# A mixture-of-experts tail on one core: another order of the eight experts, and the token dispatches moved into the short ones

## The chip, the cores and the metric

One core of a Trainium2 chip runs the whole program in one launch. The metric is the device time of one execution in microseconds. The kernel before took 1400.51 us (median of 3 runs, 1397.81 to 1400.72). A core has TensorE (PE in the profile; its weight loads are PEld), VectorE (DVE), ScalarE (ACT), GpSimd (POOL), SyncE (SP, which here issues nearly all transfers) and 16 DMA engines that move data from HBM to the on-chip memory.

## The reference

The program is a two-layer transformer block over 256 tokens of width 1024 in float32. Layer 0 has a mixer and a dense feed-forward part, layer 1 another mixer and a mixture of experts. The change lies in the mixture alone. A router picks 2 of 8 experts for each token; each expert is a gated feed-forward network of width 3584, applied to the tokens that chose it, and the results are added with the router's weights:

```python
logits = jnp.dot(xt, w_router) + b_router
top_logit, top_e = lax.top_k(logits, TOP_K)          # TOP_K = 2
gate = jax.nn.softmax(top_logit, axis=-1)
...
h = x_pad[toks]                                      # tokens of expert e
return (jax.nn.silu(h @ w_gate[e]) * (h @ w_up[e])) @ w_down[e]
...
y = jnp.zeros((N + 1, D), F32).at[slot_tok].add(y_slots * slot_gate)[:N]
```

The result is added to the scaled residual and goes through a last layer norm. Which expert has how many tokens is known only at run time.

## The kernel before

**Experts in turn.** All weights of all eight experts are read, 3 matrices of 1024 x 3584 in float32 for each. They come in loads of 512 KB (128 partitions x 1024 floats): 28 each of gate, up and down weights, 84 loads an expert and 672 in all. Expert 0 is called N here (`None` in the code). The other seven are sorted by their token counts at run time, and are called by rank, 0 with the most tokens to 6 with the fewest. `ORDER` (line 985) is the order in which they are computed.

**Short and long ones.** Experts in `FEW` (line 986: N and ranks 3 to 6) are computed with room for 64 tokens, straight from the float32 weights: the two halves of the stationary operand's 64 columns go side by side, gate in one and up in the other (`gate_up_small`, `down_small`). They are called short here. Ranks 0, 1 and 2, the long ones, have room for 128 tokens, and each weight tile is split into a high part by ScalarE (`wh`, line 150) and a low part by VectorE (`wl`, line 152), of which TensorE makes three products (`mm3`, lines 164 to 166).

**Chunks.** `experts` (line 1198) goes through an expert in four chunks of the width 3584 (1024, 1024, 1024, 512). In each chunk it computes gate and up (`pgu`, or `pg` and `pu`), and then the down product `y` of the chunk before. So the last four down loads of an expert are used after the first sixteen gate and up loads of the next one, and the next expert's second chunk also holds the `combine` (line 1179) that adds the finished expert to the sum.

**Dispatch.** Before an expert can start, its tokens must be gathered on TensorE: a matrix of zeros and ones `d` picks them out of the tokens (`xeps`), with a few transposes (`dps`) and the router's weights (`gp`). `dispatch` (line 1002) does it for one or two long experts, `dispatch_small` (line 1041) for a short one. The dictionary in line 1243 says after the second chunk of which expert (by place in `ORDER`) which others (by place too) are dispatched. While TensorE does that, it takes no weights.

**The order on the engines.** `products_in_order` (line 60) fixes TensorE's order to the order of the code; the other engines' order comes from a scheduler. SyncE issues the loads in the order in which TensorE uses them.

**The buffers.** A load goes to one of 25 buffers in turn (4 of `NRAW`, 21 of `NRAW2`; ten more of another pool are lent once, at the start). It is issued when the buffer's last user is done: a matmul for a short expert, VectorE's `wl` for a long one. So SyncE can be at most 25 loads ahead of what has been used up.

Of the kernel before, what the change touches and what calls it, by code (L numbers as in the profile page):

```python
# [8 lines left out]
F32 = mybir.dt.float32  # L9
# [8 lines left out]
P = 128  # L18
# [21 lines left out]
def hybrid_kernel(ctx, tc, x, ev_w_in, ev_w_out, dif_lambda, dif_subln, ffd_w_gate, ffd_w_up, ffd_w_down,  # L40
# [6 lines left out]
    def mkpool(name, bufs=1, side="left", **kw):  # L47
        return tc.tile_pool(name=name, bufs=bufs, side=side, reuse_waits="tile", **kw)
# [10 lines left out]
    @contextmanager  # L59
    def products_in_order():  # L60

        traced = nc.cur_bb.bb.instructions
        last = traced[-1]
        yield
        start = next(k for k in reversed(range(len(traced))) if traced[k] is last) + 1
        todo = [i for i in traced[start:] if i.engine == mybir.EngineType.PE]
        for a, b in zip(todo, todo[1:]):
            tc.add_manual_dep(b, a.name, mybir.DependencyInfo(mybir.DependencyClass.NoSync,
                                                              mybir.DependencyReason.DATA), reason="in order")
# [67 lines left out]
    def behind(ins):  # L137
        return tc.issue_after(ins) if ins is not None else nullcontext()
# [183 lines left out]
    def evac(dst, src):  # L322
        flip[0] ^= 1
        if flip[0]:
            nc.scalar.copy(dst, src)  # L325
        else:
            nc.vector.tensor_copy(dst, src)  # L327
# [355 lines left out]
    with tc.issue_after(turned):  # L683
# [15 lines left out]
        for q in range(4):  # L699
            r = slice(q * 32, q * 32 + 32)  # L700
# [240 lines left out]
    mp = ctx.enter_context(mkpool("moe"))  # L941

    def trb(shape, name):
        return tr.tile(list(shape), F32, tag="tr", name=name)
# [37 lines left out]


    SMALL = 64
    ORDER = (None, 0, 3, 1, 4, 2, 5, 6)
    FEW = (None, 3, 4, 5, 6)

    MORE = [(r, SMALL if r in FEW else P) for r in ORDER] + [(None, SMALL + P)]
    over = mp.tile([P, len(MORE) + 1], F32, name="over")
# [9 lines left out]
    def columns(r):  # L999
        return (posm[:, :, 0:1], weight[:, :, 0:1]) if r is None else (posr[:, :, r:r + 1], weightr[:, :, r:r + 1])  # L1000

    def dispatch(rs):


        n = len(rs)
        d = mp.tile([P, NT, 2, P], F32R, tag="d", name="d", bufs=1)
        for t in range(NT):
            for i, (r, base) in enumerate(rs):
                nc.vector.tensor_scalar(d[:, t, i], iota, float(base - 4096), columns(r)[0][:, t],
                                        op0=ALU.add, op1=ALU.is_equal)  # L1010
        xe = []
        for src, nm in ((xh, "xeh"), (xl, "xel")):
            dst = [mp.tile([P, KD, P], F32R, tag=nm, name=nm, bufs=2) for _ in range(n)]
            for k0 in range(0, KD, 2):
                ps = trb((P, 2, n, P), "xeps")
                for k in range(2):
                    for t in range(NT):
                        nc.tensor.matmul(ps[:, k], src[:, t, (k0 + k) * P:(k0 + k + 1) * P], d[:, t, :n],
                                         start=t == 0, stop=t == NT - 1)
                for i in range(n):  # L1020
                    evac(dst[i][:, k0:k0 + 2], ps[:, :, i])
            xe.append(dst)
        ps = trb((P, 4, P), "dps")
        for i in range(n):
            for t in range(NT):
                nc.tensor.transpose(ps[:, 2 * i + t], d[:, t, i].bitcast(F32), ident)
        gp = trb((P, 2), "gp")
        for i, (r, base) in enumerate(rs):
            for t in range(NT):
                nc.tensor.matmul(gp[:, i:i + 1], d[:, t, i].bitcast(F32), columns(r)[1][:, t],  # L1030
                                 start=t == 0, stop=t == NT - 1)
        gs = mp.tile([P, 2], F32, tag="gs", name="gs", bufs=3)
        nc.vector.tensor_copy(gs[:, :n], gp[:, :n])
        res = {}
        for i, r in enumerate(rs):
            dT = mp.tile([P, NT, P], F32R, tag="dT", name="dT", bufs=4)
            evac(dT, ps[:, 2 * i:2 * i + 2])
            res[r] = ([(xe[0][i][:, k], xe[1][i][:, k]) for k in range(KD)], gs[:, i:i + 1], dT)
        return res

    def dispatch_small(r, first):


        d = mp.tile([P, NT, P], F32 if first else F32R, tag="d", name="d_s", bufs=1)
        for t in range(NT):
            for h in range(2):
                last = nc.vector.tensor_scalar(d[:, t, h * SMALL:(h + 1) * SMALL], iota[:, 0:SMALL], -4096.0,
                                               columns(r)[0][:, t], op0=ALU.add, op1=ALU.is_equal)
        marks["d"] = last.ins
        xs = mp.tile([P, KD, SMALL], F32, tag="xs", name="xs", bufs=2)  # L1050
        srcs = (x3,) if first else (xh, xl)
        for k0 in range(0, KD, 4):
            ps = trb((P, 4, SMALL), "xeps")
            for k in range(4):
                for t in range(NT):
                    for j, src in enumerate(srcs):
                        nc.tensor.matmul(ps[:, k], src[:, t, (k0 + k) * P:(k0 + k + 1) * P], d[:, t, 0:SMALL],
                                         start=t == 0 and j == 0, stop=t == NT - 1 and j == len(srcs) - 1)
            evac(xs[:, k0:k0 + 4], ps)
        gp = trb((P, 1), "gp")  # L1060
        for t in range(NT):
            nc.tensor.matmul(gp, d[:, t].bitcast(F32), columns(r)[1][:, t], start=t == 0, stop=t == NT - 1)
        gs = mp.tile([P, 2], F32, tag="gs", name="gs", bufs=3)
        nc.vector.tensor_copy(gs[:, 0:1], gp)
        ps = trb((P, NT, P), "dps")
        for t in range(NT):
            nc.tensor.transpose(ps[:, t], d[:, t].bitcast(F32), ident)
        dT = mp.tile([P, NT, P], F32R, tag="dT", name="dT", bufs=4)
        evac(dT, ps)
        return {(r, 0): (xs, gs[:, 0:1], dT)}  # L1070
# [4 lines left out]
    def weights_of(e):  # L1075

        ws = (moe_w_gate, moe_w_up, moe_w_down)
        if isinstance(e, int):
            return [w[0, e] for w in ws]
        return [w[0, bass.ds(e, 1)].rearrange("o d f -> (o d) f") for w in ws]  # L1080
# [117 lines left out]
    def experts(runs, groups, small, disp):  # L1198

        turns, pend = [], []  # L1200

        def mid():
            while turns:
                turns.pop(0)()

        for p, (r, base) in enumerate(runs):
            if r is None:
                e = 0
            else:
                with behind(loads[-1] if p else None):  # L1210
                    e = nc.values_load(idxi[0:1, r:r + 1], engines=(mybir.EngineType.SP,), min_val=1, max_val=NE - 1)
            ws = weights_of(e)
            sm = r in small
            xe, gs, dT = disp.pop((r, base))
            ys = [yp.tile([P, 512], F32, tag="y", name="y") for _ in range(1 if sm else 2)]
            for i, (c0, n) in enumerate(CHUNKS):
                hs = (gate_up_small if sm else gate_up)(ws, c0, n, xe, mid)
                for f in pend:
                    f()
                ts = []  # L1220
                turns.append(lambda ts=ts, hs=hs, sm=sm: ts.extend((turn_small if sm else turn)(hs)))
                pend = [lambda ws=ws, c0=c0, n=n, ts=ts, ys=ys, sm=sm: (down_small if sm else down)(ws, c0, n, ts, ys)]
                if i == 1:
                    for q in groups.get(p, ()):
                        if runs[q[0]][0] in small:
                            disp.update(dispatch_small(runs[q[0]][0], False))
                        else:
                            disp.update(dispatch([runs[n_] for n_ in q]))
            pend.append(lambda ys=ys, gs=gs, dT=dT, p=p: turns.append(
                lambda: combine(ys, gs, dT, p == 0 and bool(small))))  # L1230
        mid()
        for f in pend:
            f()
        mid()

    disp = dispatch_small(None, True)
# [3 lines left out]
        with tc.issue_after(marks["d"]):  # L1240
            nc.vector.tensor_tensor(xl[:, t], x3[:, t], xh[:, t].bitcast(F32), ALU.subtract)
    with products_in_order():
        experts([(r, 0) for r in ORDER], {0: ((1, 3),), 1: ((2,),), 3: ((4,),), 4: ((5,),), 5: ((6,),), 6: ((7,),)}, FEW, disp)
    def tokens_over(i):
        return nc.values_load(overi[0:1, i:i + 1], min_val=0, max_val=S)

# [8 lines left out]
    for t in (1, 0):  # L1255
        z = acc[:, t]
        mu, r = layer_stats(z)
# [50 lines left out]
```

## Time and profile before

| | |
|---|---|
| time, median of 3 runs | 1400.51 us |
| the profiled execution's own time | 1402.62 us |
| its span, first to last instruction | 1400.8 us |
| TensorE busy | 1314.0 us (94%) |
| VectorE, ScalarE busy | 754.3 us (54%), 544.7 us (39%) |
| read from HBM | 427.64 MB |
| the experts' part of the span | from about 519 us to about 1380 us |

The profile is of one execution. The page cuts the span in 40 slices of 35 us; in its row of GB/s, the slices of the experts' part read between 329 and 409. Times below are counted from the span's start. "Busy" for TensorE counts a matmul from its start to its modelled end, so matmuls that follow each other overlap, and a stretch can be busy though TensorE waits for weights.

### The profile page before, as it was taken

The numbers are of one execution on the slowest core, as the hardware profiler recorded it, in microseconds if no ns is written. First come the engines' busy times: TensorE is split into PE (matmuls) and PEld (weight loads), VectorE is DVE, ScalarE is ACT, GpSimd is POOL, SyncE is SP. The second block draws the span as 40 slices with busy tenths as digits, with TensorE's granted clock in tenths as the row PEclk, the third lists the DMA queues.
The fourth block names the chain that finished last, engine by engine and source line by source line (L and its number), as shares of the span: only waits on it lengthen the run. The fifth ranks groups of instructions, "written<-read, shape, count | busy, mean of one in ns | idle before, by whom it ended". The sixth has DMA issues, their size and how long they took to land. (4 is left out here: it accounts for less than half of the span.)

```text
span 1400.8 us, 18207 instructions
## 1 busy us (share of the span) xinstructions
PE 1314.0 (94%) x6136; PEld 848.2 (61%) x6136; DVE 754.3 (54%) x1194; ACT 544.7 (39%) x796; POOL 45.2 (3%) x79
## 2 busy tenths in 40 slices
PE   8979999998988989999999999999998999999983
PEld 7856888886864763367874356884446886432221
DVE  5977655547578561278863057893137895201004
ACT  4454444433436311166652056772034774100000
POOL 2200000001210000000000000000000000000000
PEclk9999999999999989999999999999999999999996
DMA  9244646545543399899999999999999998999992
GB/s 348 74 135 137 225 149 211 181 121 178 161 150 121 124 362 399 333 408 409 402 355 399 402 409 409 401 408 384 405 406 409 407 389 329 409 402 409 409 402 108
DMA packets 146805, 429.98 MB, mean 307 GB/s; under 512 B 15696, under 2 KB 23280, under 8 KB 146704
## 3 DMA queue, kind: packets, MB, share of 16 engines
q1 hardware_dynamic: 146000, 426.48, 80.3%
q0 software_dynamic: 704, 2.26, 0.5%
q8 instruction: 50, 0.82, 0.2%
q14 instruction: 51, 0.42, 0.1%
HBM read 427.64 MB, written 1.05 MB: 306 GB/s over the span
## 5 line engine op out<-in xcount | busy, mean ns | idle before, releaser
L152 DVE TENSOR_TENSOR wl<-raw,wh 128x1024 fp32r<-128x1024 f32 x378 | 456.0, 1225 | 116.0 <-ACT wh L150 113.0
L150 ACT CAST wh<-raw 128x1024 fp32r<-128x1024 f32 x378 | 390.1, 1046 | 230.1 <-PE pg L166 67.7
L1124 PE MATMUL pgu<-raw,xs 128*64 128x512 f32 x1120 | 267.4, 608 | 5.1 <-DMA raw<-in_moe_w_up_dram 4.3
L1124 PEld LDWEIGHTS pgu<-raw,xs 128*64 128x64 f32 x1120 | 81.7, 139 | 166.6 <-issue 130.1
L1169 PE MATMUL y<-raw,hT_s 128*64 128x512 f32 x560 | 132.9, 605 | 6.8 <-DMA raw<-in_moe_w_down_dram 5.9
L1132 DVE TENSOR_TENSOR h_s<-h_s,pgu 64x512 f32<-64x512 f32 x35 | 24.1, 690 | 185.3 <-ACT h_s L1131 185.1
L1169 PEld LDWEIGHTS y<-raw,hT_s 128*64 128x64 f32 x560 | 37.9, 138 | 95.3 <-issue 61.7
L1131 ACT ACTIVATE h_s<-pgu 64x512 f32<-64x512 f32 x35 | 20.7, 590 | 175.7 <-PE pgu L1124 175.7
L164 PE MATMUL mmps<-wh,xTh 128*128 128x512 f32 (+2 forms) x192 | 77.4, 404 | 1.0 <-ACT wh L150 0.8
L166 PE MATMUL mmps<-wh,xTl 128*128 128x512 f32 (+2 forms) x192 | 76.2, 399 | 1.8 <-DVE xTl L173 1.7
L165 PE MATMUL mmps<-wl,xTh 128*128 128x512 f32 (+2 forms) x192 | 75.0, 393 | 0.5 <-DVE wl L152 0.5
L164 PE MATMUL pg<-wh,xeh 128*128 128x512 f32 x168 | 71.0, 422 | 1.9 <-ACT wh L150 1.6
L165 PE MATMUL pg<-wl,xeh 128*128 128x512 f32 x168 | 69.3, 413 | 2.3 <-DVE wl L152 2.3
L166 PE MATMUL pg<-wh,xel 128*128 128x512 f32 x168 | 68.8, 409 | 0.0
L164 PE MATMUL y<-wh,hTh 128*128 128x512 f32 x168 | 66.6, 396 | 0.8 <-ACT wh L150 0.8
L165 PE MATMUL y<-wl,hTh 128*128 128x512 f32 x168 | 66.5, 396 | 0.9 <-DVE wl L152 0.8
L166 PE MATMUL pu<-wh,xel 128*128 128x512 f32 x168 | 66.8, 398 | 0.0
L165 PE MATMUL pu<-wl,xeh 128*128 128x512 f32 x168 | 66.7, 397 | 0.0
L166 PE MATMUL y<-wh,hTl 128*128 128x512 f32 x168 | 66.3, 394 | 0.0
L164 PE MATMUL pu<-wh,xeh 128*128 128x512 f32 x168 | 65.4, 389 | 0.0
L327 DVE COPY hT_s<-tps 128x256 f32<-128x256 f32 x17 | 7.2, 424 | 101.5 <-PE tps L1151 101.5
L325 ACT COPY hT_s<-tps 128x256 f32<-128x256 f32 x18 | 6.7, 372 | 135.1 <-PE tps L1151 135.1
(376 smaller groups left out, 1912.8 us busy)
## 6 DMA issues: line engine op xcount, KB each, us to landing
raw<-in_moe_w_up_dram SPq DMA_DIRECT2D x224, 512.0 KB, 10.1
raw<-in_moe_w_gate_dram SPq DMA_DIRECT2D x224, 512.0 KB, 10.1
raw<-in_moe_w_down_dram SPq DMA_DIRECT2D x224, 512.0 KB, 10.1
raw<-in_ffd_w_gate_dram SPq DMA_DIRECT2D x22, 512.0 KB, 5.1
raw<-in_ffd_w_up_dram SPq DMA_DIRECT2D x22, 512.0 KB, 4.4
raw<-in_ffd_w_down_dram SPq DMA_DIRECT2D x22, 512.0 KB, 4.7
raw<-in_ev_w_in_dram SPq DMA_DIRECT2D x20, 512.0 KB, 8.9
raw<-in_od_w_in_dram SPq DMA_DIRECT2D x20, 512.0 KB, 4.2
```

The source lines that it names most:

```text
L150: nc.scalar.copy(wh[:, :w], rv)
L152: nc.vector.tensor_tensor(wl[:, :w], rv, wh[:, :w].bitcast(F32), ALU.subtract)
L164: nc.tensor.matmul(ps, ah, wh, start=first and i == 0, stop=False)
L165: nc.tensor.matmul(ps, ah, wl, start=False, stop=False)
L166: nc.tensor.matmul(ps, al, wh, start=False, stop=last and i == n - 1)
L325: nc.scalar.copy(dst, src)
L327: nc.vector.tensor_copy(dst, src)
L1124: nc.tensor.matmul(p_[i * SMALL:(i + 1) * SMALL], xs[:, k0 + k], halves(w[k], n)[j], start=k0 + k == 0, stop=k0 + k == KD - 1)
L1131: nc.scalar.activation(h[:SMALL], p_[:SMALL], AF.Silu)
L1132: nc.vector.tensor_tensor(h[:SMALL], h[:SMALL], p_[SMALL:], ALU.mult)
L1169: nc.tensor.matmul(ys[0][i * SMALL:(i + 1) * SMALL], ts[k], w[:, i * 512:(i + 1) * 512], start=c0 == 0 and k == 0, stop=c0 + n == F_EXP an ...
```

## The change

Three edits. The order becomes N 3 0 4 1 5 2 6 instead of N 0 3 1 4 2 5 6: which experts are short and which long stays the same, and so does the last one. The dispatches move: N now hosts rank 3; rank 3 hosts ranks 0 and 1 together and then rank 4; rank 4 hosts rank 5 and then rank 2; rank 5 hosts rank 6. Before, N hosted 0 and 1, rank 0 hosted 3, rank 1 hosted 4, rank 4 hosted 2, rank 2 hosted 5, and rank 5 hosted 6. And the small tile `gs`, which holds an expert's router weights until it is combined, gets 5 buffers instead of 3.

```diff
-    ORDER = (None, 0, 3, 1, 4, 2, 5, 6)
+    ORDER = (None, 3, 0, 4, 1, 5, 2, 6)
...
-        gs = mp.tile([P, 2], F32, tag="gs", name="gs", bufs=3)
+        gs = mp.tile([P, 2], F32, tag="gs", name="gs", bufs=5)
...
     with products_in_order():
-        experts([(r, 0) for r in ORDER], {0: ((1, 3),), 1: ((2,),), 3: ((4,),), 4: ((5,),), 5: ((6,),), 6: ((7,),)}, FEW, disp)
+        experts([(r, 0) for r in ORDER], {0: ((1,),), 1: ((2, 4), (3,)), 3: ((5,), (6,)), 5: ((7,),)}, FEW, disp)
```

How this moves instructions is shown at three places of TensorE's order. The first is in expert N, after its second chunk; `d` is the matrix of a long expert's dispatch, `d_s` that of a short one, `x3h` and `x3l` are the two parts of the tokens. Before:

```order
L1169 MATMUL y<-raw,hT_s 64x512 x16
L1018 MATMUL xeps<-d,x3h 128x256 x16
L1018 MATMUL xeps<-d,x3l 128x256 x16
L1026 MATMUL dps<-ident,d 128x128 x4
L1030 MATMUL gp<-weightr,d 128x1 x4
L1124 MATMUL pgu<-raw,xs 64x512 x8
L1151 MATMUL tps<-ident,h_s 128x64 x8
```

The same place in the changed kernel, from the last of 32 `xeps` matmuls of rank 3's dispatch on:

```order
L1057 MATMUL xeps<-d_s,x3l 128x64
L1062 MATMUL gp<-weightr,d_s 128x1 x2
L1067 MATMUL dps<-ident,d_s 128x128 x2
L1124 MATMUL pgu<-raw,xs 64x512 x8
L1151 MATMUL tps<-ident,h_s 128x64 x8
```

The dispatch of two long experts has gone from here, and that of a short one stands in its place. The second place is in rank 4, after its second chunk. Before:

```order
L1124 MATMUL pgu<-raw,xs 64x512 x24
L1169 MATMUL y<-raw,hT_s 64x512 x16
L1018 MATMUL xeps<-d,x3h 128x128 x16
L1018 MATMUL xeps<-d,x3l 128x128 x16
L1026 MATMUL dps<-ident,d 128x128 x2
L1030 MATMUL gp<-weightr,d 128x1 x2
L1124 MATMUL pgu<-raw,xs 64x512 x8
```

The same place in the changed kernel, again from the last of the 32 on:

```order
L1057 MATMUL xeps<-d_s,x3l 128x64
L1062 MATMUL gp<-weightr,d_s 128x1 x2
L1067 MATMUL dps<-ident,d_s 128x128 x2
L1018 MATMUL xeps<-d,x3h 128x128 x16
L1018 MATMUL xeps<-d,x3l 128x128 x16
L1026 MATMUL dps<-ident,d 128x128 x2
L1030 MATMUL gp<-weightr,d 128x1 x2
L1124 MATMUL pgu<-raw,xs 64x512 x8
```

A short expert's dispatch has been put in ahead of the long one's, with no weights used in between. The third place is the middle of a long expert, between the second chunk's `pu` and `y` and the third chunk's `pg`. Before, in rank 0:

```order
L1057 MATMUL xeps<-d_s,x3l 128x64
L1062 MATMUL gp<-weightr,d_s 128x1 x2
L1067 MATMUL dps<-ident,d_s 128x128 x2
L164 MATMUL pg<-wh,xeh 128x512
L165 MATMUL pg<-wl,xeh 128x512
L166 MATMUL pg<-wh,xel 128x512
```

The same place in the changed kernel:

```order
L164 MATMUL y<-wh,hTh 128x512
L165 MATMUL y<-wl,hTh 128x512
L166 MATMUL y<-wh,hTl 128x512
L164 MATMUL pg<-wh,xeh 128x512
L165 MATMUL pg<-wl,xeh 128x512
L166 MATMUL pg<-wh,xel 128x512
```

No dispatch stands in a long expert any more: the third chunk follows the down products directly.

## Rows read from the trace of the kernel before

**Rows 1.** Windows: us; busy time (and count) by engine; PEclk, DMA share, GB/s

```profile
564.00:576.00 12.00, 12.00 (x65) 4.79 (x66) 1.66 (x7) 0.64 (x2) 0.00 (x0) 1.00 0.67 223
576.00:726.00 150.00, 148.47 (x671) 106.95 (x668) 111.19 (x109) 93.02 (x100) 0.00 (x0) 0.98 1.03 405
726.00:741.00 15.00, 15.00 (x71) 7.17 (x71) 3.17 (x4) 2.48 (x3) 0.00 (x0) 1.00 0.77 274
...
1160.00:1186.00 26.00, 26.00 (x117) 15.92 (x117) 13.12 (x12) 10.04 (x11) 0.00 (x0) 1.00 0.84 304
1186.00:1370.00 184.00, 172.16 (x742) 59.27 (x738) 22.73 (x36) 15.08 (x27) 0.00 (x0) 0.99 1.03 405
```

**Rows 2.** SyncE's longest wait in 555:572, then in 1160:1186 (total us, times, longest)

```profile
SPq L131 <- PE pgu L1124: 11.1, 2, 9.5
...
SPq L131 <- PE pgu L1124: 9.1, 5, 5.9
```

**Rows 3.** Timeline of TensorE: three dispatches (0 and 1; 2; 6), and what follows

```profile
556.56 1.22 PE L1018 MATMUL xeps<-d,x3h 128*128 128x256 f32 x8
...
564.68 3.65 PE L1124 MATMUL pgu<-raw,xs 128*64 128x512 f32 x16
...
997.47 2.29 PE L1018 MATMUL xeps<-d,x3h 128*128 128x128 f32 x16
...
1003.57 6.58 PE L1124 MATMUL pgu<-raw,xs 128*64 128x512 f32 x16
...
1220.75 0.30 PE L1057 MATMUL xeps<-d_s,x3h 128*128 128x64 f32 x1
...
1225.63 4.79 PE L1124 MATMUL pgu<-raw,xs 128*64 128x512 f32 x16
```

**Rows 4.** Timeline of TensorE: first weight matmuls of N, 0, 3, 1, 4, 2, 5, 6

```profile
518.83 4.91 PE L1124 MATMUL pgu<-raw,xs 128*64 128x512 f32 x16
...
600.75 0.50 PE L164 MATMUL pg<-wh,xeh 128*128 128x512 f32 x1
...
730.67 3.65 PE L1124 MATMUL pgu<-raw,xs 128*64 128x512 f32 x16
...
815.93 0.51 PE L164 MATMUL pg<-wh,xeh 128*128 128x512 f32 x1 [1.60 <-ACT wh L150]
...
949.88 2.37 PE L1124 MATMUL pgu<-raw,xs 128*64 128x512 f32 x10
...
1042.56 0.50 PE L164 MATMUL pg<-wh,xeh 128*128 128x512 f32 x1
...
1175.37 1.94 PE L1124 MATMUL pgu<-raw,xs 128*64 128x512 f32 x8
...
1262.73 3.60 PE L1124 MATMUL pgu<-raw,xs 128*64 128x512 f32 x16
```

**Rows 5.** Timeline of SyncE: issue of the first load of 3, 1, 4, 2, 5, 6

```profile
691.91 0.34 SPq L131 DMA_DIRECT2D raw<-in_moe_w_gate_dram  x1
...
804.36 0.33 SPq L131 DMA_DIRECT2D raw<-in_moe_w_gate_dram  x1
...
914.32 0.33 SPq L131 DMA_DIRECT2D raw<-in_moe_w_gate_dram  x1
...
1024.53 0.70 SPq L131 DMA_DIRECT2D raw<-in_moe_w_gate_dram  x1
...
1136.60 0.33 SPq L131 DMA_DIRECT2D raw<-in_moe_w_gate_dram  x1
...
1249.22 0.34 SPq L131 DMA_DIRECT2D raw<-in_moe_w_gate_dram  x1
```

**Rows 6.** Window behind rank 2's dispatch, columns as in the first rows

```profile
1003.60:1010.10 6.50, 6.50 (x18) 1.71 (x17) 0.81 (x5) 0.00 (x0) 0.00 (x0) 0.55 1.02 405
```

**Rows 7.** The last load of all: line 131 in 1363:1364, issue and landing

```profile
L131 SPq DMA_DIRECT2D raw<-in_moe_w_down_dram x1: 333/333/333, 1363.2 to 1363.2; - x1
...
DMA to landing us min/median/max: 11.5/11.5/11.5
```

More of the change, by code (lines that the diff above doesn't have):

```diff
@@ L1062, in dispatch_small @@
             nc.tensor.matmul(gp, d[:, t].bitcast(F32), columns(r)[1][:, t], start=t == 0, stop=t == NT - 1)
-        gs = mp.tile([P, 2], F32, tag="gs", name="gs", bufs=3)
+        gs = mp.tile([P, 2], F32, tag="gs", name="gs", bufs=5)
         nc.vector.tensor_copy(gs[:, 0:1], gp)
```

## The prediction

> **What bounds the kernel now.** I read the windows of the experts' part first, for the rate of the transfers. It is 405 GB/s in the long stretches, with a DMA share of 1.03, and 223, 274 and 304 GB/s in three short ones [rows 1]. TensorE's busy time cannot tell that: it is 172.16 of 184 us in the last stretch, where it follows the loads, and all of 26 us in one where it holds them up. So the bound is the stream of weights, 672 loads, and what can be won are the stretches in which it stalls. Against 405 GB/s they lose 12 x (1 - 223/405) = 5.4 us, 15 x (1 - 274/405) = 4.9 us and 26 x (1 - 304/405) = 6.5 us, 16.8 us in all [rows 1].
>
> Next SyncE's waits: in the first and the third of these stretches its longest waits, 9.5 and 5.9 us, are for a `pgu` matmul of TensorE [rows 2]. It waits for a buffer: it is 25 loads ahead, and TensorE has not used the oldest. The first stall comes while TensorE does the dispatch of ranks 0 and 1, from 556.56 to 564.68 us, and uses no weights for 8.1 us [rows 3]. The other two come where a short expert begins after a long one: rank 3 at 730.67 and rank 5 at 1175.37 us [rows 4].
>
> To see why there and not behind rank 1, I take for each expert the lead: from the issue of its first load [rows 5] to its first weight matmul [rows 4].
>
> - rank 3: 730.67 - 691.91 = 38.8 us, a stall of 4.9 us behind it
> - rank 1: 815.93 - 804.36 = 11.6 us; TensorE waits for the load here ("ACT wh", 1.60 us), so this is the floor
> - rank 4: 949.88 - 914.32 = 35.6 us, no stall
> - rank 2: 1042.56 - 1024.53 = 18.0 us
> - rank 5: 1175.37 - 1136.60 = 38.8 us, a stall of 6.5 us
> - rank 6: 1262.73 - 1249.22 = 13.5 us
>
> So up to 35.6 us the stream does not stall. The lead is cut off at 38.8 us, and what would go beyond turns into stall. An unhindered expert's 84 loads take 1024.53 - 914.32 = 110.2 us [rows 5]. TensorE needs more than that for a long expert (the lead grows) and less for a short one (it shrinks). For rank 2 the lead would have grown from 18.0 by 132.8 - 110.2 = 22.6 us to 40.6; it went with a stall of 6.5 us. Between the two points a stall of 6.5/(40.6 - 35.6) = 1.3 us belongs to each us above 35.6.
>
> **The change part by part.** First the prices of the dispatches [rows 3]: two long ones 564.68 - 556.56 = 8.1 us, one long 1003.57 - 997.47 = 6.1 us, one short 1225.63 - 1220.75 = 4.9 us. The matmuls that follow can be slow: 16 of them take 3.65 us at best, 4.79 after the short dispatch (1.1 more), 6.58 after the long one (2.9 more). All dispatches are the same in number and kind before and after, so only their places count.
>
> *The first stall.* N loses a dispatch of 8.1 us and gets one of 4.9 us. The buffer comes free 3.2 us earlier, less 0 to 1.1 us for slow matmuls: 2.2 to 3.3 us of the 5.4 stay. I take 2.7.
>
> *Rank 3 in the second place.* N takes 600.75 - 518.83 - 8.1 + 4.9 + 1.1 = 79.8 us, so rank 3 begins at 598.6 us. A short expert without a dispatch is 87.4 - 4.9 - 1.1 = 81.3 us (rank 5, 1175.37 to 1262.73, less its dispatch). With its two dispatches rank 3 takes at most 81.3 + 8.1 + 4.9 + 1.1 = 95.4 us, to 694.0 us. Rank 0's first load is the one now issued at 691.91 us, in the same place of the stream, 2.7 us earlier; with the floor of 11.6 us it is used at 700.8 us. So TensorE waits for loads, 6.8 us are to spare, the 13 us of dispatch cost nothing, and rank 0 begins at the floor. With that cover gone they would be paid in lead, one for one.
>
> *Rank 0, now without a dispatch.* Rank 2's 132.8 us less 4.9 are 127.9 us, so a long expert adds 17.7 us: from 11.6 to 29.3. No stall: 4.9 us saved.
>
> *Rank 4 with two dispatches.* It takes 92.7 us now (949.88 to 1042.56), with rank 2's dispatch and the slow matmuls in it. The short dispatch adds 4.9 to 6.0 us: 98.7 us, and the lead falls by 11.5, to 17.8. VectorE's rows for it stand ahead in its order or take under 1 us between the two; I leave that in the bound.
>
> *Rank 1* then ends at 17.8 + 17.7 = 35.5 us, just at the point where stalls begin. From below this costs 0; from above, if the second dispatch too ran at half speed (6.1 us more), 41.6 us and 1.3 x 6.0 = 7.8 us. I take 1.5, since the nearest row is rank 4's start now, at the same 35.6 us and without a stall.
>
> [...]
>
> *Rank 5, rank 2, rank 6.* Rank 5 takes off 110.2 - 87.4 = 22.8 (35.5 to 12.7), rank 2 adds 17.7 (30.4, no stall: 6.5 us saved), and rank 6 takes off 110.2 - 81.3 = 28.9, more than there is. So TensorE ends waiting for loads, as now, with the same last expert behind them. The tail from the last load's landing at 1363.2 + 11.5 = 1374.7 us [rows 7] to the end is not touched.
>
> *`gs` with 5 buffers* costs nothing on any queue; it lets four dispatched experts wait.
>
> The sum: stalls of 16.8 us become 2.7 + 0 + 1.5 + 0 = 4.2, a gain of 12.6 us. The profiled execution would go from 1402.62 to 1390.0 us. It lay 2.1 us above the median shown, so for that I say 1388.0 us.
>
> **The rivals.**
>
> *Given back behind rank 1.* The clock falls for the whole of rank 4's double dispatch: 7.8 us of stall in place of 1.5, so 1394.3. For it: [rows 6] and the lead of 35.5, which has no room. Against it: rank 5's dispatch slowed the next matmuls by 1.1 us alone.
>
> *No stall at all.* Long experts take less than 127.9 us once their middle is not broken: then rank 1's end lies below 35.6, and if the first stall goes too, the time is 1400.5 - 16.8 = 1383.7; with 2.7 of it left, 1386.4. For it: rank 0 now needs 129.9 us with its dispatch (600.75 to 730.67), 3 less than rank 2. Against it: rank 0 follows N, whose result is the first and is not added to a sum; all three long ones now follow a short expert whose is.
>
> *It doesn't do what it says.* If rank 3 does not run into its loads, rank 0 begins above the floor, and all leads behind it rise. It needs 13 us more there (6.8 to spare and 6.3 up to 35.6), and about 10 beyond for today's stalls: 1400. Nothing in the rows asks for 23 us in a short expert.
>
> *Slower: TensorE becomes the bound.* With two short experts first it idles early, and one short expert alone is left to catch up at the end. From 700.8 us it has 3 x 127.9 + 98.7 + 87.4 + 81.3 = 651.1 us to do, to 1351.9; the last load lands at 1374.7 - 12.6 = 1362.1. So 10 us are to spare. From 10 us of extra work on, the end moves with TensorE; from 23 on, the kernel is slower than before. Three long experts of 134 us (rank 1's time now, 815.93 to 949.88, with a dispatch) and 6 us in rank 4 would make 18 + 6 = 24: about 1402 us. Against it: 4.9 us of the 134 are the dispatch that leaves.
>
> **How the numbers follow.** The forecast 0.62, given back 0.20, no stall 0.08, not what it says 0.05, slower 0.05. What a measurement of this kernel can tell from no change is about 0.2%, 2.8 us. The first three are faster by more: 0.90; then the same 0.05 and slower 0.05. The range from 1383.5 (no stall) to 1396 (given back, with 1.5 us of run to run) leaves out the last two and little else.
>
> **What would show it.** In the profile after: a short low-rate stretch of about 2 to 3 us lost near 560 us; none where rank 4 and rank 6 begin; at most a small one where rank 5 begins (near 1050 us); rank 3 (second) with TensorE waiting for loads before rank 0 starts near 701 us; leads near 29, 35 and 30 us at the ends of ranks 0, 1 and 2; rates near 405 GB/s from 700 us on; and the last load landing near 1362 us. I am wrong if a stall of 5 us stands behind rank 1 or inside rank 4, if rank 0 starts well after 701 us, or if TensorE does not wait for loads in rank 6's last chunks.

## The result, and the profile after

The changed kernel takes 1390.28 us (median of 5 runs, 1388.07 to 1393.63) against 1400.72 us: ratio 0.9923, 95% interval 0.9906 to 0.994. It is faster, by 10.4 us; 1388.0 us had been forecast. Its profiled execution is the longest of the five: 1393.63 us, a span of 1391.9 us. A later set gave the same kernel 1391.35 us against 1399.53 (0.9941, 0.992 to 0.9962).

The windows of the kernel after (columns as in [rows 1]) show where the stream of weights still stalls:

```profile
562.00:578.00 16.00, 16.00 (x76) 5.52 (x74) 1.60 (x3) 1.55 (x3) 0.00 (x0) 0.91 0.86 310
...
890.00:906.00 16.00, 15.98 (x72) 6.83 (x73) 2.08 (x8) 0.74 (x2) 0.00 (x0) 0.82 0.64 216
906.00:1057.00 151.00, 148.14 (x650) 104.86 (x646) 108.61 (x102) 90.91 (x99) 0.00 (x0) 0.98 1.03 407
1057.00:1070.00 13.00, 13.00 (x63) 4.55 (x64) 0.69 (x1) 0.58 (x1) 0.00 (x0) 1.00 0.89 331
1070.00:1340.00 270.00, 260.24 (x1192) 151.12 (x1190) 136.38 (x140) 110.20 (x127) 0.00 (x0) 0.99 1.03 407
```

Against 405 GB/s they lose 16 x (1 - 310/405) = 3.8 us at N's dispatch, 16 x (1 - 216/405) = 7.5 us inside rank 4 and 13 x (1 - 331/405) = 2.4 us behind rank 1. Behind rank 0 and rank 2, where [rows 1] had 4.9 and 6.5 us, nothing is lost. SyncE's waits in the three places (555 to 575, 885 to 905, 1055 to 1070 us; total, times, longest) have the same partner as in [rows 2]:

```profile
SPq L131 <- PE pgu L1124: 12.2, 5, 8.2
...
SPq L131 <- PE pgu L1124: 13.2, 4, 10.7
...
SPq L131 <- PE pgu L1124: 8.3, 6, 4.8
```

The middle one is new, and longer than those of [rows 2]. TensorE's timeline at the four dispatch places, answering to [rows 3], shows why (N; rank 3, two long and then a short one; rank 4, a short and then a long one; rank 5):

```profile
554.37 0.30 PE L1057 MATMUL xeps<-d_s,x3h 128*128 128x64 f32 x1
559.41 6.31 PE L1124 MATMUL pgu<-raw,xs 128*64 128x512 f32 x16
...
644.97 1.21 PE L1018 MATMUL xeps<-d,x3h 128*128 128x256 f32 x8
653.64 0.39 PE L1057 MATMUL xeps<-d_s,x3h 128*128 128x64 f32 x1 [0.51 <-DVE d_s L1047]
661.91 6.26 PE L1124 MATMUL pgu<-raw,xs 128*64 128x512 f32 x16
...
878.64 0.30 PE L1057 MATMUL xeps<-d_s,x3h 128*128 128x64 f32 x1
884.13 3.67 PE L1018 MATMUL xeps<-d,x3h 128*128 128x128 f32 x16 [0.38 <-DVE d L1009]
892.63 5.26 PE L1124 MATMUL pgu<-raw,xs 128*64 128x512 f32 x16
...
1105.04 0.30 PE L1057 MATMUL xeps<-d_s,x3h 128*128 128x64 f32 x1
1109.63 3.65 PE L1124 MATMUL pgu<-raw,xs 128*64 128x512 f32 x16
```

Rank 4's two dispatches take 892.63 - 878.64 = 14.0 us, rank 3's 661.91 - 644.97 = 16.9 us. The windows of rank 4's, and of the 16 matmuls behind them, have the clock:

```profile
878.60:892.60 14.00, 13.61 (x78) 12.77 (x76) 3.19 (x9) 2.23 (x6) 0.00 (x0) 0.63 0.94 370
892.60:897.90 5.30, 5.30 (x18) 1.52 (x19) 0.81 (x5) 0.00 (x0) 0.00 (x0) 0.69 0.14 29
```

The granted clock is 0.63 and 0.69, and while those 16 matmuls run, the loads all but stop: 29 GB/s. So the place to look at is not only the start of an expert but also where TensorE takes up its weights again behind a dispatch. A low GB/s alone is not yet a loss of that size, as the second profile below shows; here the loads behind the pause did land late.

First-load issues and first weight matmuls of ranks 0, 4, 1 and 5, as [rows 5] and [rows 4]:

```profile
686.84 0.33 SPq L131 DMA_DIRECT2D raw<-in_moe_w_gate_dram  x1
...
795.89 0.33 SPq L131 DMA_DIRECT2D raw<-in_moe_w_gate_dram  x1
...
911.64 0.33 SPq L131 DMA_DIRECT2D raw<-in_moe_w_gate_dram  x1
...
1019.86 0.34 SPq L131 DMA_DIRECT2D raw<-in_moe_w_gate_dram  x1
```

```profile
700.59 0.50 PE L164 MATMUL pg<-wh,xeh 128*128 128x512 f32 x1
...
827.75 3.65 PE L1124 MATMUL pgu<-raw,xs 128*64 128x512 f32 x16
...
930.29 0.50 PE L164 MATMUL pg<-wh,xeh 128*128 128x512 f32 x1
...
1057.01 3.65 PE L1124 MATMUL pgu<-raw,xs 128*64 128x512 f32 x16
```

The leads are 13.8, 31.9, 18.7 and 37.2 us. From rank 4's first load to rank 1's pass 911.64 - 795.89 = 115.8 us, 5.6 more than the 110.2 that [rows 5] gave for an unhindered expert, and 6.7 and 7.5 more than the 109.1 and 108.2 us of ranks 0 and 1 here. One wait has grown besides: behind each of the three long experts TensorE idles before its last down products (5.0 us on ScalarE in three waits), since ScalarE does the short expert's silu ahead of the casts for them. Before, one such wait of 0.79 us on ScalarE is in the trace. The one in rank 4:

```profile
844.09 0.49 PE L164 MATMUL y<-wh,hTh 128*128 128x512 f32 x1 [1.65 <-ACT wh L150]
845.35 0.79 PE L165 MATMUL y<-wl,hTh 128*128 128x512 f32 x1 [0.77 <-DVE wl L152]
```

The down products behind it run at a granted clock of 0.57 (844 to 849 us).

The last load is issued at 1354.1 us and lands 11.5 us later ([rows 7]: 1363.2 and 11.5). The part ahead of the experts differs by some us from one execution to the next, so I measure from N's first weight matmul to the last landing: 855.9 us before (518.83 to 1374.7), 850.2 after (515.41 to 1365.6).

### The profile page after: what moved, and what is told of

Same layout as the page of the kernel before. It is cut to its first block, busy times and chain, and to the rows that moved or that the text cites. A ratio compares the mean times of both kernels' runs of the same rounds, so it can differ in the third digit from the quotient of the medians.

```text
span 1391.9 us, 18210 instructions
## 1 busy us (share of the span) xinstructions
PE 1306.8 (94%) x6136; PEld 851.5 (61%) x6136; DVE 753.0 (54%) x1194; ACT 543.4 (39%) x796; POOL 48.9 (4%) x79
## 5 line engine op out<-in xcount | busy, mean ns | idle before, releaser
L1124 PE MATMUL pgu<-raw,xs 128*64 128x512 f32 x1120 | 260.9, 614 | 0.0
L1169 PE MATMUL y<-raw,hT_s 128*64 128x512 f32 x560 | 127.6, 595 | 5.1 <-DMA raw<-in_moe_w_down_dram 3.5
```

The costliest lines, as they stand in the source:

```text
L1124: nc.tensor.matmul(p_[i * SMALL:(i + 1) * SMALL], xs[:, k0 + k], halves(w[k], n)[j], start=k0 + k == 0, stop=k0 + k == KD - 1)
L1169: nc.tensor.matmul(ys[0][i * SMALL:(i + 1) * SMALL], ts[k], w[:, i * 512:(i + 1) * 512], start=c0 == 0 and k == 0, stop=c0 + n == F_EXP an ...
```

## The experiments

The theories they set against each other: A, TensorE's work is paid only up to the last place where the stream waits for it, and a stall that goes earlier comes back there; B, each stall is a loss of its own; C, the moved dispatches carry the gain; E, the clock falls. This table has all runs. "Stretch" is the time from N's first weight matmul to the last landing in the one profiled execution. Each ratio is to the kernel before as timed in the same set (medians of 1399.07 to 1400.72 us). The sets did not all run on the same chip, so the ratios compare kernels of different sets better than the medians do. Of the edits to line 1243 the dictionary alone is shown below; a key in brackets is (place, chunk), both counted from 0, and goes with the change of the code shown for N's dispatch.

| kernel | stretch, us | median, us (runs) | ratio to before, 95% |
|---|---|---|---|
| before | 855.9 | 1400.72 (5) | |
| after | 850.2 | 1390.28 (5) | 0.9923 (0.9906 to 0.994) |
| after, again | 843.2 | 1391.35 (9) | 0.9941 (0.992 to 0.9962) |
| order only | 844.5 | 1391.16 (6) | 0.9943 (0.9924 to 0.9963) |
| dispatches only | 859.9 | 1406.92 (6) | 1.0058 (1.0041 to 1.0075) |
| N's dispatch later | 841.9 | 1391.21 (6) | 0.9946 (0.9926 to 0.9966) |
| two dispatches later | 842.4 | 1388.01 (6) | 0.9913 (0.9893 to 0.9933) |
| pairs split | 843.4 | 1388.98 (5) | 0.9914 (0.9893 to 0.9936) |
| rank 4's dispatch doubled | 851.6 | 1397.19 (12) | 0.9985 (0.9968 to 1.0002) |
| rank 6's doubled | 854.3 | 1397.54 (12) | 0.9982 (0.9962 to 1.0002) |
| split and late | 841.1 | 1387.14 (5) | 0.9906 (0.989 to 0.9922) |
| two buffers less | 847.4 | 1396.31 (11) | 0.9984 (0.9968 to 1.0) |
| casts first | 842.9 | 1389.45 (6) | 0.9927 (0.9907 to 0.9947) |
| late, rank 5's doubled | 843.2 | 1388.77 (6) | 0.9928 (0.9909 to 0.9948) |

### Which half of the change: the order alone, the dispatches alone

```
order only (in after):
-    {0: ((1,),), 1: ((2, 4), (3,)), 3: ((5,), (6,)), 5: ((7,),)}
+    {0: ((1,),), 1: ((2, 4),), 2: ((3,),), 3: ((6,),), 4: ((5,),), 6: ((7,),)}
dispatches only (in before; gs with 5 buffers):
-    {0: ((1, 3),), 1: ((2,),), 3: ((4,),), 4: ((5,),), 5: ((6,),), 6: ((7,),)}
+    {0: ((1, 3), (2,)), 2: ((4,),), 4: ((5,), (6,)), 6: ((7,),)}
```

> The new order, but the short experts' dispatches put back into the long experts ahead of them (rank 4's into rank 0, rank 5's into rank 1, rank 6's into rank 2); the two long ones, ranks 0 and 1, stay in rank 3. Theory A (one path): TensorE works without a gap from N's start to the end of the last stall, and then the loads that are left set the end; only how much of TensorE's work lies before that point counts. Then the order alone carries nearly all of the gain: no stall inside rank 4, since it starts at a lead near 35 us with one long dispatch, as before the change, where it had none; a stall of about 8 us behind rank 1, whose lead grows by rank 5's dispatch to some 42 us; 3.8 us at N's dispatch. Sum 11.8 us against 13.2 us after the change: 1389 us (1386 to 1392). Theory C (the moved dispatches carry the gain, each long expert that loses one saves 5 us of stall): about 1396 us or more.

> The order of before (N 0 3 1 4 2 5 6), but the short experts' dispatches moved into short experts: rank 3's from rank 0 to N, rank 4's from rank 1 to rank 3, rank 5's from rank 2 to rank 4, where rank 2's stands already. Theory A (one path): every dispatch that moves was before the last stall (behind rank 2) and still is, so the stalls change places and little in sum: 5 us more at N's dispatches, 4 us less behind rank 0, 7 us new inside rank 4, 6.5 us less behind rank 2. 1402 us (1399 to 1406). Theory C (the moved dispatches carry the gain): 1390 to 1394 us.

The order alone has the whole gain, 1391.16 us. Its stalls did not come where A had put them: rank 5 started at a lead of 34.0 us, not 42, and the window behind rank 1 (348 GB/s over 16 us) lost 2.3 us, not 8. The dispatches alone are slower than before, by 0.6%: C falls. In that kernel N does a pair and a short one in a row, 16.4 us, and the loads stand still meanwhile:

```profile
560.00:576.00 16.00, 14.91 (x72) 11.26 (x74) 3.91 (x16) 1.96 (x6) 0.00 (x0) 0.68 0.12 46
```

That is 16 x (1 - 46/405) = 14.2 us lost where before lost 5.4. A's sum was 4.9 us short: I had counted 5 us more at N, and it is 8.8.

### Is a stall a loss of its own: N's dispatch later

```
-                if i == 1:
-                    for q in groups.get(p, ()):
+                if True:
+                    for q in groups.get((p, i), ()):
...
+    {(0, 2): ((1,),), (1, 1): ((2, 4), (3,)), (3, 1): ((5,), (6,)), (5, 1): ((7,),)}
```

> The kernel after, with N's dispatch (of rank 3) traced in N's third chunk of four, not in its second. The stall of 3.8 us at 562 to 578 us goes in both theories. Theory B (stalls add up, each is a loss of its own): 1386.5 us, 3.8 us less than after. Theory A (one path): rank 3 ends when TensorE is through with N and rank 3, no earlier; the loads run 3 to 4 us further ahead, rank 0's lead grows from 13.8 to about 17 us and rank 4's from 31.9 to about 35 us, and the stall inside rank 4 grows by the same 3 to 4 us: 1390 us, no change within 1.5 us.

The stall at N's dispatch is gone from the profile, and the time is 1391.21 us, that of the kernel after. That speaks for A, but does not settle it. B's 1386.5 us takes off the 3.8 us of one execution; with the 2.5 us that the stall has in the second profile below, B says about 1389 us (from the 1391.35 of that set), which the interval of about 2.8 us either way leaves open. And the leads did not go A's way: rank 0 began at 11.2 us, the floor, not at 17, and rank 4 at 30.5, not 35.

### Where a dispatch costs nothing: two of them later

```
-    {0: ((1,),), 1: ((2, 4), (3,)), 3: ((5,), (6,)), 5: ((7,),)}
+    {0: ((1,),), 1: ((2, 4), (3,)), 3: ((5,),), 5: ((6,),), 6: ((7,),)}
```

> The kernel after, with two dispatches moved later: rank 2's from rank 4 to rank 5, rank 6's from rank 5 to rank 2. Rank 4 keeps rank 5's short one alone. Theory A (one path): some 9.4 us of dispatch and the slow matmuls behind it, 2 us, now come after the point of the last stall. No stall inside rank 4, rank 1 starts at a lead of about 14 us and ends at 31 to 32, no stall behind it; rank 5 with one long dispatch comes down to 15; rank 2 with rank 6's dispatch ends at 37 to 38, a stall of about 2 us behind it. 3.8 + 2 us of stall against 13.2: 1383 us (1381 to 1386). Theory D (not the dispatch: rank 4 stalls because of what follows a long expert there, the idle time of TensorE before the long expert's last down products and the slow matmuls): the stall inside rank 4 stays over 4 us and the time over 1387 us.

1388.01 us. Inside rank 4 and behind rank 1 no stall is left: rank 4 starts at a lead of 29.6 us and rank 1 at 11.2. Besides N's dispatch, one low place remains, where rank 6 starts at a lead of 34.6 us; a stall of about 2 us had been expected there:

```profile
1268.00:1284.00 16.00, 16.00 (x76) 6.23 (x76) 0.69 (x1) 0.63 (x2) 0.00 (x0) 1.00 0.86 322
```

D had the stall stay, and it is gone with the idle time before the down products still there, so D falls as it was put; the profile of casts first, below, has the dispatches and not the idle time, and no stall either. The gain is 2 to 3 us, not 7, and the time lies 2.0 us outside A's range: my 13.2 us of stall came from one execution that had more of it than most, as the next run shows.

### The same kernel again, and the pairs split

> The changed kernel once more, for a second profile of it and six more times. Every theory: 1390 us (1388 to 1393). What it is to show is which of its stretches differ from one execution to the next. Theory E (the clock falls by chance behind a single dispatch and always behind two in a row): the two double dispatches, in ranks 3 and 4, take 13 us or more again, and the 16 matmuls behind them over 5 us; the single ones in N and rank 5 take 4.6 to 5.9 us, with 3.65 us or over 5 us behind them, either.

In this execution the pair in rank 4 took 13.1 us and the lead at its start was 29.4 us. TensorE's timeline at N and rank 4, then the first-load issues of ranks 4 and 1 on SyncE, then the window behind the pair:

```profile
553.66 0.30 PE L1057 MATMUL xeps<-d_s,x3h 128*128 128x64 f32 x1
558.31 3.65 PE L1124 MATMUL pgu<-raw,xs 128*64 128x512 f32 x16
...
870.94 0.30 PE L1057 MATMUL xeps<-d_s,x3h 128*128 128x64 f32 x1
884.09 5.21 PE L1124 MATMUL pgu<-raw,xs 128*64 128x512 f32 x16
```

```profile
793.51 0.33 SPq L131 DMA_DIRECT2D raw<-in_moe_w_gate_dram  x1
...
903.70 0.33 SPq L131 DMA_DIRECT2D raw<-in_moe_w_gate_dram  x1
```

```profile
884.00:900.00 16.00, 16.00 (x73) 5.57 (x75) 1.23 (x6) 0.78 (x2) 0.00 (x0) 0.90 0.95 346
```

Behind N's dispatch the 16 matmuls take 3.65 us where they took 6.31: the same code, at a granted clock of 1.00 (560 to 576 us) where it was 0.57 (559.4 to 565.7 us). From rank 4's first load to rank 1's pass 110.2 us, not 115.8, and the stretch is 7 us shorter. By its GB/s this window still loses 2.3 us. The loads say less. SyncE's last issue before the pause behind the pair and its first one behind it, with the time to their landing, in the first execution and in this one:

```profile
884.60 0.39 SPq L131 DMA_DIRECT2D raw<-in_moe_w_gate_dram  x1
DMA to landing us min/median/max: 10.5/10.5/10.5
896.20 0.38 SPq L131 DMA_DIRECT2D raw<-in_moe_w_up_dram  x1
DMA to landing us min/median/max: 3.7/3.7/3.7
...
882.26 0.39 SPq L131 DMA_DIRECT2D raw<-in_moe_w_gate_dram  x1
DMA to landing us min/median/max: 10.5/10.5/10.5
887.60 0.38 SPq L131 DMA_DIRECT2D raw<-in_moe_w_up_dram  x1
DMA to landing us min/median/max: 6.5/6.5/6.5
```

In the first, a pause of 11.6 us puts the landings nearly 5 us apart (895.1 and 899.9). In the second, a pause of 5.3 us leaves them 1.3 us apart (892.8 and 894.1), as loads land where nothing holds them up: those in flight covered it. So the GB/s of a window can show a stall where the loads land in time, and where a stall taken from a window is short, its size here is an upper bound.

So the kernel after sits on an edge. In the five profiles with this pair, 25 buffers and the casts in their old place, the pause behind it grows with the lead at which rank 4 started: 5.3 us at 29.4 (this one), 6.5 at 30.5 (N's dispatch later), 8.6 at 30.8 (rank 6's doubled), 11.6 at 31.9 (the first) and 12.3 at 36.6 (rank 4's doubled); the landings around it are 1.3, 1.3, 1.8, 4.9 and 5.7 us apart. In the first profile N took 82.6 us, with the slow matmuls behind its dispatch, in this one 78.5. The 14 timed runs of the kernel go from 1385.98 to 1399.24 us.

Over ten profiles the 18 pairs of a short and a long dispatch in a row took 13.1 to 16.9 us (22.9 with one doubled), and the next 16 matmuls always 5.1 to 6.6. Apart, in short experts, a long one takes 5.7 to 6.1 us and a short one 4.6 to 5.9 (8.1 for two long ones together), and behind N's single one the next 16 took 3.65 us in eight profiles of ten. Hence the next kernel:

```
+    {(0, 1): ((1,),), (1, 1): ((2, 4),), (1, 2): ((3,),),
+     (3, 1): ((6,),), (3, 2): ((5,),), (5, 1): ((7,),)}
```

> The kernel after, with the same dispatches in the same experts, but not two in a row: in rank 3 the two long ones stay in the second chunk and rank 4's goes to the third; in rank 4 rank 2's stays and rank 5's goes to the third. Theory E (the clock falls for two dispatches in a row) with theory A (one path): in rank 4 14.0 us become 5.9 + 4.6, and the next 16 matmuls 3.65 instead of 5.26, 5 us less on the path; in rank 3 2 us more until rank 0 is at the floor of its lead. 1384.5 us (1382 to 1387). Without E, if two dispatches in a row cost what two single ones do: 1390 us, since under A a dispatch a chunk later only moves the stall to behind rank 1.

1388.98 us, 1386.93 to 1390.44. The long dispatch of rank 4 now takes 5.7 us and the short one 4.6, at a granted clock of 1.00 and 0.99 (windows of the two):

```profile
872.90:878.60 5.70, 5.46 (x42) 4.80 (x40) 1.70 (x4) 1.86 (x5) 0.00 (x0) 1.00 1.02 408
901.80:906.40 4.60, 4.56 (x40) 4.30 (x38) 0.58 (x2) 0.37 (x1) 0.00 (x0) 0.99 1.03 405
```

So E holds for the dispatches themselves, 3 to 4 us of rank 4's pair. For the 16 matmuls behind it does not: they take 5.35 us behind the single long one as well. In time the split is 1.3 to 2.4 us better than the kernel after, which the intervals do not tell apart, and 4.5 us above the forecast of E with A.

### The price of TensorE's work, in three places

```
-            for k in range(4):
+            for k in [0, 1, 2, 3] * (2 if r == 4 else 1):
(r == 6 in the second; r == 5, in the kernel with two dispatches later, in the third)
```

> The kernel after, with the 32 matmuls of rank 4's dispatch (in rank 3, at about 655 us) done twice over; the result is the same. They take 3.6 us at full clock and 6.8 us at the lower. Theory A (one path): TensorE's work ahead of the last stall is paid one for one: 4 to 7 us more, 1396 us (1393 to 1398). The forecast's ledger (in the second place of the order dispatches lie under the loads, 6.8 us to spare): 1390 us, no change.

> The kernel after, with the 32 matmuls of rank 6's dispatch (in rank 5, at about 1105 us, behind the last stall) done twice over; the result is the same. Theory A (one path): the same extra 3.6 to 6.8 us now lie behind the last stall, rank 2 starts at a lead of 19 to 22 us and rank 6 at 36 to 39, with a stall of 0 to 3 us only at the upper end: 1391 us (1390 to 1393). A theory by which TensorE's work costs the same wherever it stands: 1396 us.

> The kernel with rank 2's and rank 6's dispatch an expert later (run before at 1388.0 us), and in it the 32 matmuls of rank 5's dispatch, in rank 4, done twice over; the result is the same. In the two runs with a doubled dispatch so far the same work cost 6 us. Theory A (one path; work on TensorE is paid only where a lead is at its limit): in this kernel rank 4 starts at a lead of 29.6 us and rank 1 at 11.2, the floor, so there is room at both ends of the dispatch: rank 4 is 4 to 8 us longer, rank 1 starts at a lead of 13 to 18 us, rank 5 at 31 to 36, and no stall is new: 1388 us (1387 to 1390). Theory F (each doubled dispatch is paid, in this place as in the others): 1394 us.

The 3.6 and 6.8 us are read from the first profile: 32 such matmuls take 3.59 us at a granted clock of 1.00 (878.64 to 882.23 us) and 6.82 us at 0.50 (653.64 to 660.46 us).

Rank 4's doubled dispatch made its pair in rank 3 22.9 us instead of 16.4 to 16.9 and cost 5.8 us: it is paid one for one, and the 6.8 us to spare that the prediction had there are not to be had. Rank 6's cost as much, 6.2 us, against my expectation. SyncE's wait in 1108 to 1130 us and the window behind the dispatch show a stall inside rank 5, and the next window one where rank 6 starts, at a lead of 38.4 us:

```profile
SPq L131 <- PE pgu L1124: 11.9, 5, 8.9
```

```profile
1115.00:1131.00 16.00, 16.00 (x69) 5.34 (x70) 0.85 (x2) 0.37 (x1) 0.00 (x0) 0.84 0.83 303
...
1276.00:1292.00 16.00, 16.00 (x75) 7.44 (x75) 0.80 (x2) 0.59 (x1) 0.00 (x0) 1.00 0.85 313
```

Rank 5 starts at the limit of its lead (38.0 us here), so a dispatch that is 5 us longer holds up the loads at its end. I had looked at the starts of ranks 2 and 6 and not at the restart in the middle of rank 5, the omission of the prediction once more. And the last place where the stream waited was in this kernel not behind rank 1 but where rank 6 starts: its lead came to the upper end of what I had expected (36 to 39 us), and the window there loses 3.6 us. So the doubled work lay ahead of the last such place, not behind it.

The third kernel does the same doubled work where the lead has room at both ends. TensorE's timeline of it, and the window:

```profile
872.12 0.30 PE L1057 MATMUL xeps<-d_s,x3h 128*128 128x64 f32 x1
881.84 5.16 PE L1124 MATMUL pgu<-raw,xs 128*64 128x512 f32 x16
```

```profile
882.00:900.00 18.00, 18.00 (x82) 6.06 (x84) 2.24 (x5) 1.88 (x4) 0.00 (x0) 0.92 1.04 396
```

9.7 us of dispatch instead of 4.6, and 1388.77 us against 1388.01, or 2.1 us more by the ratios: not told apart from free, and below F's 1394 us (a ratio of 0.996), which its interval leaves out. Read with the restart and with rank 6's start as places of their own, A fits all three; the range that I had given for rank 6's missed by 4.5 us.

### The ring, the casts, and the two together

```
two buffers less:   -NRAW2 = 21   +NRAW2 = 19
casts first (gate_up_small):
+        after = ahead()     # loads and casts of the long expert's last down product
...
+            with behind(after):
+                nc.scalar.activation(h[:SMALL], p_[:SMALL], AF.Silu)
split and late:
+    {(0, 2): ((1,),), (1, 1): ((2, 4),), (1, 2): ((3,),),
+     (3, 1): ((5,),), (5, 1): ((6,),), (6, 1): ((7,),)}
```

> The kernel after with 23 buffers for loads in place of 25. Each lead is cut off two loads, 2.6 us, earlier. Theory A (one path): the stream is 2.6 us further back at each point at which TensorE releases it, but what is lost at one stall is not lost again at the next, since TensorE's own time does not change: 2.6 us more in a run that stalls inside ranks 4 or 5 anyhow, 1394 us (1392 to 1396). Theory B (each stall a loss of its own): three stalls of 2.6 us, 1398.5 us.

> The kernel after, with ScalarE's casts of the last four down loads of each long expert ordered ahead of the silu of the short expert that follows. The 1.65 + 0.77 us for which TensorE idles before these products in ranks 4, 5 and 6 go. Dispatches, order and loads stay. Theory A (one path): 2.4 us off the path ahead of the restart in rank 4, as much again ahead of that in rank 5, and fewer clock drops behind the idle time: 1388 us (1386 to 1390). If only the dispatches' places matter: 1391 us.

> The new order with no two dispatches in a row and as many as possible late: N's in its third chunk; in rank 3 the two long ones in the second chunk and rank 4's in the third; rank 4 with rank 5's alone, rank 5 with rank 2's alone, rank 2 with rank 6's. Theory A (one path, the lead of each expert against its limit at its start and at the restart behind its dispatch): no lead comes to 36 us but at the most rank 6's start, no stall is left anywhere, the stall at N's dispatch (1.6 to 4.6 us in the profiles so far) goes too. 1386 us (1384 to 1388), with a narrower spread than the kernel after, since a fallen clock has cover everywhere. If stalls were not what is left: 1388 to 1389 us, as with either part of it alone.

Two buffers cost 5.0 us against the repeat of the kernel after, 6.0 by the ratios, between A (2.6) and B (7.8). The stretch is 4.2 us longer than the repeat's, with a stall back inside rank 4 (window behind its pair):

```profile
891.30:907.00 15.70, 15.70 (x73) 5.42 (x75) 1.23 (x6) 0.61 (x2) 0.00 (x0) 0.90 0.76 264
```

That fits a kernel on the edge: executions that had next to no stall there now have one. It does not settle A against B, and nothing else here does: N's dispatch later leaves both open, and the doubled dispatches set A against F, by which the work costs the same wherever it stands.

With the casts first the idle time before the down products is gone, and the profile has no stall inside rank 4. 1389.45 us is 0.8 to 1.9 us better than after, too little to tell.

Split and late has the lowest median of all: 1387.14 us (1384.95 to 1389.60), 0.9906 of before, with the shortest stretch, 841.1 us. 1386 had been expected, and 1388 to 1389 if stalls were not what is left; the interval does not tell these apart. The stall at N's dispatch is gone, and one low place is left in the profile, where rank 6 starts at a lead of 37.0 us:

```profile
1268.00:1286.00 18.00, 18.00 (x84) 8.50 (x84) 1.55 (x2) 0.58 (x1) 0.00 (x0) 1.00 0.80 302
```

SyncE pauses for 6.4 us there, and the loads land 1.3, 1.4 and 2.6 us apart behind it, so little of it is lost. Against the kernel after, whose intervals overlap its own, it is 3 to 4 us better in the median, at most.

Of the eleven ranges given for A, six held the median. Two dispatches later and pairs split missed by 2.0 us, rank 6's doubled by 4.5, dispatches only by 0.9 and two buffers less by 0.3.

## Why the prediction was right, and where not

- *The bound and the gain.* Right: the stream of weights sets the end, and the stalls behind ranks 0 and 2 went. 12.6 us were forecast, 10.4 and 8.2 measured in two sets. In the stretch the two profiles of after gained 5.7 and 12.7 us. The sum behind the forecast came out less well than the total: it left 4.2 us of stall, and the first profile has 3.8 + 7.5 + 2.4 = 13.7. So the total is closer to the forecast than its terms are, in part by luck.
- *The first stall*, 2.7 us: 3.8 us in the profile with the fallen clock (0.57 behind the dispatch), 2.5 us in the other (341 GB/s in 560 to 576, at 1.00).
- *Rank 3 in the second place.* Rank 0 began at 700.59 us, 700.8 forecast, but that is luck: N itself began 3.4 us earlier in this execution. Counted from N's first weight matmul, rank 0 began at 185.2 us, not at 182.0. Its first load went out only 1.7 us earlier than before by this count (4.7 in the second profile), not 2.7, and TensorE came 2.1 us after the floor (lead 13.8, not 11.6). N and rank 3 took 82.6 and 102.6 us where 79.8 and 95.4 had been worked out; rank 3's three dispatches took 16.9 us where 13.0 were taken. So the 6.8 us of cover were used up, and what TensorE does there is paid; the doubled dispatch shows it.
- *A long expert's 17.7 us of lead.* Right: 31.9 - 13.8 = 18.1 and 37.2 - 18.7 = 18.5. Two errors cancel in it: TensorE took 127.2 and 126.7 us, not 127.9, and the loads 109.1 and 108.2, not 110.2.
- *Rank 4 with two dispatches*: the step that failed. I checked the leads where experts begin and took no stall inside rank 4. Behind its pair TensorE takes up the weights 14.0 us later, at a granted clock of 0.69 for 5.3 us more, and 7.5 us were lost there in the profiled execution. I had named a stall of 5 us inside rank 4 as what would prove me wrong; by that one execution I was, by the second, with 2.3 us by the window and next to nothing by the landings, not. Two things were missed: the restart as a place where the lead can hit its limit, and the size of the pair, 13.1 to 14.0 us against the 6.1 us that stood there and the 4.9 to 6.0 that I added.
- *Behind rank 1*, 1.5 us: 2.4 and 1.7 us (359 GB/s over 15 us). The rival "given back behind rank 1" had the right mechanism, the clock falling in rank 4's pair (0.63 and 0.73 in the two profiles), and the wrong place. The half speed of its second dispatch was my estimate: the granted clock was 0.50 there (884.13 to 892.63 us), but the dispatch took 8.5 us, 2.4 and not 6.1 more than in [rows 3]. Behind all 18 pairs the next 16 matmuls took over 5 us; two long dispatches alone, with four transposes, ran at a granted clock of 1.00 in all four profiles that have them, with 3.65 us for the 16 matmuls behind. No run here parts the transposes from the small matmuls.
- *The end.* Right: TensorE waits for loads in rank 6's last chunks, and nothing moved behind the last landing.
- *Not forecast at all*: that executions of one kernel differ by 7 us in the stretch. The range, 1383.5 to 1396, held both medians for the stall sizes it allowed, not for this.

## What to carry to other kernels

When a ring of buffers feeds an engine, work out how far the loads run ahead not only where a stage begins but wherever the consumer comes back from other work; here a long pause at a large lead made the stall (11.6 us at 31.9 us), and loads that landed as closely as before (1.3 us apart) showed that there was next to none, though the window read 346 GB/s. Work on the consumer cost 5.8 and 6.2 us ahead of the last such place at its limit, and 0.8 to 2.1 us where the lead had room at both ends: move such work behind the last of those places, or to where the consumer waits for loads anyway. And where one execution stalls and the next does not, take a second profile before a stall is given a size.

## What the hardware showed that I had not expected

- The granted clock behind the same short dispatch is not the same from run to run: the next 16 matmuls took 3.65 us in eight profiles and 5.9 to 6.3 us in two (granted clock 0.57 in the first profile, 1.00 in the second). Behind a short and a long dispatch in a row they took 5.1 to 6.6 us, 18 times of 18 (0.58 behind rank 3's and 0.69 behind rank 4's in the first profile).
- Behind rank 4's pair, where TensorE held the ring of buffers, the loads did not slow down but all but stopped: 29 GB/s for the 5.3 us from 892.6, and 407 GB/s from 906 us on.
- The time from the first instruction to N's first weight matmul, the same code in all kernels, went from 515.4 to 521.0 us across the profiles; where few us count, it has to be taken out.
